# A decoder trunk with split-precision projections: the weights' low half in fp32r in place of bf16

## The chip, the cores and the metric

One core of a Trainium2 chip. The metric is the device time of one execution in microseconds; a kernel is timed as the median of several runs, and one further execution is profiled.

## What is computed

Two layers on one sequence of 256 positions of width 1024, all in float32. Layer 0 puts one input projection in front of two groups of heads (forgetting attention and retention), multiplies their outputs by a gate and projects them back. Layer 1 is sparse attention with a compressed, a selected and a window branch, a gate and an output projection. Each layer starts with an RMS norm and adds its input; a last norm ends it.

```python
h = rms_norm(x, norm_g); u = h @ w_in                      # layer 0
q_f, k_f, v_f, f_l, q_r, k_r, v_r, z = jnp.split(u, EVEN_SPLITS, axis=-1)
...
y = jnp.concatenate([o_f, o_r], axis=-1) * jax.nn.silu(z)
x = x + y @ w_out
...
h = rms_norm(x, norm_g); u = h @ w_in                      # layer 1
q, kc, vc, ks, vs, kw, vw, gl, z = jnp.split(u, ODD_SPLITS, axis=-1)
...
return jax.nn.silu(ab @ w1) @ w2                           # compress_blocks, for keys and for values
...
x = x + (o * jax.nn.silu(z)) @ w_out
```

## The kernel before

**Split products.** Each large product is made of three smaller ones, so that it keeps more digits than one fast product would. An operand is written as a high half (rounded to fp32r, a float32 that TensorE multiplies at a fast rate) and a low half (what the rounding left). The class `Split` holds an activation h so: `h` and `l` in fp32r, and `b`, a bf16 copy of the high half. ScalarE writes `h`, VectorE (for x0 and x1, L119) or GpSimd (for y0 and y1, L102) writes `l`, GpSimd copies `b` (L99). The weights come in 38 chunks of 256 to 280 columns: SyncE loads a chunk (1 MB) into a stage tile `st` (three buffers); `split` cuts it in four quarters, ScalarE rounding each into `wh` (fp32r, L95) and VectorE subtracting it into `wl` (bf16, L102). The product is `wh` with `h`, `wh` with `l` and `wl` with `b`.

**Units.** A chunk holds two units. A unit is one output tile of 128 rows, with 8 slices k of the sum and three matmuls for each: 24 matmuls into one PSUM bank, 256 columns each. `mtile` takes the weights as the stationary operand (matmul at L211), `vtile` the activations (L218). `runs` writes out the order: for `runs(4, 4)` it is `wh` with `h` and `l` for k = 0 to 3, then `wl` with `b` for the same four k, then the same for k = 4 to 7. A unit is handed out in eight steps of three matmuls.

**The order of the work.** `Feed` has the list of all steps; the attention code calls `feed.run(n)` between its own parts, so that TensorE has projection work while the other engines make softmax and norms. The numbers n are written out by hand (`FR`, `RR`, `HW`, `NR` and so on). A chunk's quarters are split when the step counter is within `LEAD` = 22 steps of its start (four steps apart), and the last quarter issues the next load that is free. This program order is then the priority of a list scheduler, which fixes the order on every engine and on SyncE's queue ahead of the run; at run time every engine takes its instructions in that order.

**The turn between the layers.** The output projection of layer 0 (`pp_o`) adds to `xT` (VectorE, L380), from which `put_scaled` makes x1 and `Norm.add` a running sum of squares (`acc_n`, GpSimd). R, the norm's factor, is there when the last tile is summed. Then the compression keys and values follow (`kc`, `vc`): VectorE multiplies by R and writes `ab`, the blocks, in 32 pieces; `ph` (L707) multiplies `ab` with the compression weights `w` in eight rounds of four products, with three feed steps between rounds. Each round needs 256 KB for keys and the same for values: `load_w1` has eight loads of 512 KB into two buffers of their own, the first two ahead of the rounds, the others each after the round that frees a buffer.

Of the kernel before, what the change touches and what calls it, by code (L numbers as in the profile page):

```python
# [25 lines left out]
for _name, _w in (("U", 512), ("onehot", 8), ("mask", 384), ("ident", 128), ("bones", 128),  # L26
# [5 lines left out]
WMAX = 280  # L32
# [12 lines left out]
N0 = (5, 0, 8, 0, 0, 9)  # L45
LEAD = 22

E = dict(whi="AAAA", wlo="VVVV", xhi="AAAAAAAA", x0hi="AAAVAAAV", w0hi="AAAV", xb="G", sq="A", acc="G", yhi="A", ylo="G", yb="G", sz="G",
         q2h="AA", q2l="GG", a0="A", a1="V", ac="V", norm="GGGG", pn="G", kh="AA", kl="VV", ab="VVVV", pT="A", cs="GG", tree="VGG", xg="AAAAAAAA")
FIN = (("V", 0, 1), ("G", 1, 1), ("V", 2, 2), ("G", 4, 1), ("V", 5, 3))  # L50

# [2 lines left out]
def trunk_kernel(ctx: ExitStack, tc: tile.TileContext, a: dict):  # L54
    nc = tc.nc
    V, A, G, T = nc.vector, nc.scalar, nc.gpsimd, nc.tensor
# [36 lines left out]
    def copy(e, o, x):  # L93
        if e == "A":
            A.activation(o, x, AF.Copy)  # L95
        elif e == "V":
            V.tensor_copy(o, x)
        else:
            G.tensor_scalar(o, x, 1.0, 1.0, op0=OP.mult, op1=OP.mult)  # L99
# [11 lines left out]
    class Split:  # L111
        def __init__(s, name, tag):
            s.h = cp.tile([P, KT, S], F32R, tag=tag + "h", name=name + "h")
            s.l = cp.tile([P, KT, S], F32R, tag=tag + "l", name=name + "l")
            s.b = cp.tile([P, KT, S], BF, tag=tag + "b", name=name + "b")

        def put_scaled(s, k, x, g, e="xhi"):
            scale(E[e][k], s.h[:, k], x, g)
            V.scalar_tensor_tensor(s.l[:, k], x, g, s.h[:, k].bitcast(F32), op0=OP.mult, op1=OP.subtract)  # L119
            copy(E["xb"], s.b[:, k], s.h[:, k].bitcast(F32))  # L120

        def put(s, k, y):
            copy(E["yhi"], s.h[:, k], y)
            binary(E["ylo"], s.l[:, k], y, s.h[:, k].bitcast(F32), OP.subtract)
            copy(E["yb"], s.b[:, k], s.h[:, k].bitcast(F32))

# [1 line left out]
    class Feed:  # L130
# [22 lines left out]
        def split(s):  # L153

            i, q = divmod(s.cut, 4)
            c = s.chunks[i]
            n, st = c["n"], c["st"]
            if q == 0:
                c["w"] = (whp.tile([P, KT, WMAX], F32R, tag="wh", name=f"wh{i}"),
                          wlp.tile([P, KT, WMAX], BF, tag="wl", name=f"wl{i}"))  # L160
            wh, wl = c["w"]
            k = slice(2 * q, 2 * q + 2)
            copy(E["whi" if i else "w0hi"][q], wh[:, k, :n], st[:, k, :n])
            binary(E["wlo"][q], wl[:, k, :n], st[:, k, :n], wh[:, k, :n].bitcast(F32), OP.subtract)
            s.cut += 1
            if q == 3 and s.loaded < len(s.chunks):
                s.load()
# [11 lines left out]

    feed = Feed()  # L180

    def runs(*lengths):

        seq, k0 = [], 0
        for n in lengths:
            seq += [(w, k) for k in range(k0, k0 + n) for w in "hl"] + [("b", k) for k in range(k0, k0 + n)]
            k0 += n
        assert k0 == KT
        return seq

    def products(kind, name, done, seq, one):

        def make(c):
            o = []

            def step(i):
                if i == 0:
                    o.append(bank(kind, "pp_" + name))
                for n in range(3 * i, 3 * i + 3):
                    one(c, o[0], *seq[n], n == 0, n == 3 * KT - 1)  # L200
                if i == KT - 1:
                    done(c, o[0])
            return step
        return make

    def mtile(col, xs, kind, name, done, seq=runs(4, 4)):

        def one(c, p, w, k, start, stop):
            x = xs() if callable(xs) else xs
            wt = c["w"][w == "b"]  # L210
            T.matmul(p[:, :S], wt[:, k, col * P:col * P + P], dict(h=x.h, l=x.l, b=x.b)[w][:, k], start=start, stop=stop)  # L211
        return products(kind, name, lambda c, p: done(p[:, :S]), seq, one)

    def vtile(tt, x, kind, name, done, seq=runs(4, 4)):

        def one(c, p, w, k, start, stop):
            wt, n = c["w"][w == "b"], c["n"]
            T.matmul(p[:, :n], dict(h=x.h, l=x.l, b=x.b)[w][:, k, tt * P:tt * P + P], wt[:, k, :n], start=start, stop=stop)  # L218
        return products(kind, name, lambda c, p: done(p[:, :c["n"]]), seq, one)

    class Norm:

# [114 lines left out]
    def forget_sum():  # L337
# [5 lines left out]
        for i in (32, 96):  # L343
            V.tensor_tensor(CC[i:i + 8], pc[i:i + 8, :S], CC[i:i + 8].bitcast(F32), op=OP.subtract)

    feed.chunk(a["w0v0"], 264, [vtile(tt, x0, "p", f"v0_0{tt}", v0_done(0, tt), runs(*[1] * KT)) for tt in range(2)],
               [(tt, k) for k in range(KT) for tt in range(2)])
    for c in range(1, 4):
        feed.chunk(a["w0c"][c - 1], 256, [vtile(tt, x0, "s" if c == 1 else "p", f"v0_{c}{tt}", v0_done(c, tt)) for tt in range(2)])
# [35 lines left out]
    def out_chunks(w, y, done, nm, wide, early):  # L385

        units = []
        for m in range(8):
            units.append(mtile(m % 2, y, "p" if m < 2 or m >= wide else "s", f"{nm}{m}", done(m),
                               runs(*((4, early - 4, 8 - early) if m < wide else (4, 4)))))  # L390
        start = len(feed.steps)
        for c in range(4):
            feed.chunk(w[c], 256, units[2 * c:2 * c + 2])
        st = feed.steps[start:]
        step = lambda m, k: st[m * 8 + k]
        order = [(m, k) for m in range(wide) for k in range(early)]
        order += [(m, k) for k in range(early, 8) for m in range(wide)]
        order += [(m, k) for m in range(wide, 8) for k in range(8)]
        feed.steps[start:] = [step(m, k) for m, k in order]
        for c in range(4):  # L400
            feed.chunks[-4 + c]["start"] = start + min(i for i, (m, k) in enumerate(order) if m // 2 == c)
# [64 lines left out]
    def v1_done(c, tt):  # L466
        def done(p):
# [4 lines left out]
            if tt == 1:  # L472
# [2 lines left out]
                V.tensor_scalar(g0, g0, C("rowm"), None, op0=OP.mult)  # L475
        return done

    feed.chunk(a["w1c"][0], 256, [mtile(0, x1, "s", "kc0", c00_done, runs(4, 3, 1)), mtile(1, x1, "s", "kc1", c_done(0, 1), runs(4, 3, 1))],
               [(u, k) for u in range(2) for k in range(7)] + [(0, 7), (1, 7)])
    feed.chunk(a["w1c"][1], 256, [mtile(u, x1, "p", f"vc{u}", c_done(1, u)) for u in range(2)])  # L480
    feed.chunk(a["w1c"][2], 256, [mtile(u, x1, "s", f"ks{u}", ks_done(0, u)) for u in range(2)])
# [29 lines left out]
            v1_chunk(1)  # L511
            feed.steps += q1_steps

    y1 = Split("y1", "y")
    x2 = xT

    def o1_done(m):
# [156 lines left out]
    sq = None  # L674
# [19 lines left out]
    w1 = {}  # L694

    def load_w1(i):
        w1[i] = wk.tile([P, 2, 2, 256], F32, tag="w1", name=f"w1_{i}")
        nc.sync.dma_start(w1[i], a["wkv1"][:, :, 2 * i:2 * i + 2].rearrange("v p j n -> p v j n"))

    load_w1(0)  # L700
    load_w1(1)
# [2 lines left out]
    for qr in range(8):  # L704
        for j in range(2):
            for kv in range(2):
                T.matmul(ph[64 * kv:64 * kv + 64, :256], ab[:, kv, 2 * qr + j].rearrange("p g c -> p (g c)"),  # L707
                         w1[qr][:, kv, j], start=(qr == 0 and j == 0), stop=(qr == 7 and j == 1))
        if qr < 6:
            load_w1(qr + 2)  # L710
        feed.run(HW[1 + qr])
    hid = wk.tile([P, 256], F32, tag="y", name="hid")
    hs = wk.tile([P, 256], F32, tag="kc", name="hs")
# [21 lines left out]
    for u in range(2):  # L735
# [266 lines left out]
```

## Time and profile before

| | us |
|---|---|
| median of 3 runs | 320.18 (318.6 to 321.68) |
| the profiled execution: its time | 321.15 |
| its span, from the first instruction to the last | 319.4 |
| TensorE busy | 301.4 |
| VectorE busy | 226.6 |
| ScalarE busy | 202.5 |
| GpSimd busy | 125.2 |

Busy times are unions of an engine's instructions; matmuls overlap in the pipeline, so a high busy share of TensorE doesn't say how fast the matmuls follow each other. The mean granted clock of TensorE is 0.984 of 2.4 GHz. PE is TensorE, PEld its weight loads, DVE VectorE, ACT ScalarE, POOL GpSimd, SP SyncE.

### The profile page before, as it was taken

What the parts mean: (1) busy time and instruction counts of PE and PEld (TensorE: products, weight loads), DVE (VectorE), ACT (ScalarE), POOL (GpSimd) and SP (SyncE); (2) the same over time, 40 slices, a digit from 0 to 9 for tenths busy, and PEclk for the clock granted to TensorE, in tenths of its full rate; (3) what the DMA queues carried; (4) which work ended last, traced back from release to release, by engine and by line L of the source; (5) the groups of instructions that cost most, each with busy time, mean ns of one, the idle gap of its engine ahead of it and who ended that gap; (6) DMA issues with size and microseconds to landing.
All of it is one profiled execution on the core that took longest, in us unless ns stands there. A gap on an engine that the chain in (4) does not pass through costs nothing.

```text
span 319.4 us, 6788 instructions
## 1 busy us (share of the span) xinstructions
PE 301.4 (94%) x2478; PEld 263.4 (82%) x2478; DVE 226.6 (71%) x686; ACT 202.5 (63%) x547; POOL 125.2 (39%) x202
## 2 busy tenths in 40 slices
PE   6989999999999999999959989999999999999990
PEld 4879988988888888988947767997998899888980
DVE  2988955665656555299998937798978898883433
ACT  4759456666645456287425628598988898891461
POOL 2520020542423115284100000367778777973242
PEclk9799999999999999999997999999999999999997
DMA  6997799754343433408717992226322442100003
GB/s 178 365 308 248 262 389 307 250 174 133 131 134 131 134 133 133 131 6 269 263 29 253 303 331 73 84 70 196 133 63 72 135 131 68 67 2 0 3 0 131
DMA packets 43137, 49.72 MB, mean 156 GB/s; under 512 B 1632, under 2 KB 39776, under 8 KB 42848
## 3 DMA queue, kind: packets, MB, share of 16 engines
q1 hardware_dynamic: 42816, 49.03, 46.9%
q8 instruction: 19, 0.31, 0.4%
q10 hardware_dynamic: 288, 0.26, 0.2%
q14 instruction: 14, 0.11, 0.1%
HBM read 48.24 MB, written 1.05 MB: 154 GB/s over the span
## 4 chain that ended last, share of the span: by engine, by line
PE 54%; DVE 21%; ACT 15%; DMA 4%; issue 3%; POOL 1%; DVEq 0%; SPq 0%; ACTq 0%; POOLq 0%
PE pp_o L211 10%; ACT p L782 9%; PE pp_q L211 8%; DVE wl L102 7%; PE pp_k L211 7%; PE pp_z L211 7%; PE pp_v L218 5%; DVE ab L102 3%; PE ph L707 2%; DMA w<-in_wkv_dram 2%; PE pp_kc L211 2%; PE pp_kw L211 2%; ACT wh L95 2%; ACT q L95 2%; DMA xT<-in_xT_dram 1%
## 5 line engine op out<-in xcount | busy, mean ns | idle before, releaser
L102 DVE TENSOR_TENSOR wl<-st,wh 128x512 bf16<-128x512 f32 (+2 forms) x152 | 107.2, 736 | 10.3 <-ACT wh L95 9.7
L95 ACT ACTIVATE wh<-st 128x512 fp32r<-128x512 f32 (+2 forms) x151 | 87.7, 621 | 37.9 <-PE pp_o L211 8.1
L108 POOL TENSOR_SCALAR p<-p,st 128x128 f32<-128x128 f32 (+1 forms) x80 | 44.7, 576 | 49.5 <-DVE st L598 31.2
L211 PEld LDWEIGHTS <-wl 128*128 128x128 bf16 x512 | 40.1, 98 | 11.1 <-issue 2.1
L782 ACT ACTIVATE p<-ns,st 128x128 f32<-128x128 f32 (+1 forms) x64 | 28.4, 445 | 7.7 <-DVE st L770 7.6
L102 POOL TENSOR_TENSOR q<-q,q 64x256 fp32r<-64x256 f32 x16 | 12.1, 756 | 48.2 <-ACT q L95 47.2
L218 PE MATMUL pp_v<-wh,x0h 128*128 128x256 f32 (+1 forms) x64 | 19.9, 337 | 1.9 <-ACT wh L95 1.9
L770 DVE CUSTOM_DVE_ANT_0 ns<-s,cst 128x128 f32<-128x128 f32 (+1 forms) x64 | 20.1, 350 | 0.0
L211 PE MATMUL pp_o<-y0h,wh 128*128 128x256 f32 x64 | 17.8, 308 | 0.7 <-DVE xT L380 0.7
L211 PE MATMUL pp_z<-x0h,wh 128*128 128x256 f32 x64 | 18.1, 309 | 0.0
L211 PE MATMUL pp_q<-x0h,wh 128*128 128x256 f32 x64 | 17.7, 308 | 0.0
L211 PE MATMUL pp_q<-x1h,wh 128*128 128x256 f32 x64 | 17.6, 303 | 0.0
L211 PE MATMUL pp_k<-x0h,wh 128*128 128x256 f32 x64 | 17.2, 302 | 0.0
L218 PE MATMUL pp_v<-wh,x0l 128*128 128x256 f32 (+1 forms) x64 | 17.0, 291 | 0.0
L211 PE MATMUL pp_o<-y1h,wh 128*128 128x256 f32 x64 | 16.9, 303 | 0.0
L211 PE MATMUL pp_o<-y1l,wh 128*128 128x256 f32 x64 | 16.9, 289 | 0.0
L211 PE MATMUL pp_z<-x0l,wh 128*128 128x256 f32 x64 | 16.6, 286 | 0.0
L211 PE MATMUL pp_z<-x1h,wh 128*128 128x256 f32 x64 | 16.6, 292 | 0.0
L211 PE MATMUL pp_q<-x1l,wh 128*128 128x256 f32 x64 | 16.1, 280 | 0.0
L211 PE MATMUL pp_o<-y0l,wh 128*128 128x256 f32 x64 | 16.1, 281 | 0.0
L211 PE MATMUL pp_q<-x0l,wh 128*128 128x256 f32 x64 | 16.0, 280 | 0.0
L211 PE MATMUL pp_k<-x0l,wh 128*128 128x256 f32 x64 | 15.9, 281 | 0.0
(322 smaller groups left out, 907.1 us busy)
## 6 DMA issues: line engine op xcount, KB each, us to landing
st<-in_w0c_dram SPq DMA_DIRECT2D x13, 1024.0 KB, 5.7
st<-in_w1c_dram SPq DMA_DIRECT2D x12, 1024.0 KB, 5.7
w<-in_wkv_dram SPq DMA_DIRECT2D x8, 512.0 KB, 5.7
st<-in_w0o_dram SPq DMA_DIRECT2D x4, 1024.0 KB, 5.7
st<-in_w1o_dram SPq DMA_DIRECT2D x4, 1024.0 KB, 5.5
st<-in_w1v_dram SPq DMA_DIRECT2D x2, 1120.0 KB, 5.0
st<-in_w0c_dram SPq DMA_DIRECT2D x4, 512.0 KB, 8.1
dec<-in_dec_dram SPq DMA_DIRECT2D x2, 768.0 KB, 8.8
```

What stands on the lines that cost most here:

```text
L95: A.activation(o, x, AF.Copy)
L102: (V if e == "V" else G).tensor_tensor(o, x, y, op=op)
L108: (V if e == "V" else G).tensor_scalar(o, x, c, 1.0, op0=OP.mult, op1=OP.mult)
L211: T.matmul(p[:, :S], wt[:, k, col * P:col * P + P], dict(h=x.h, l=x.l, b=x.b)[w][:, k], start=start, stop=stop)
L218: T.matmul(p[:, :n], dict(h=x.h, l=x.l, b=x.b)[w][:, k, tt * P:tt * P + P], wt[:, k, :n], start=start, stop=stop)
L707: T.matmul(ph[64 * kv:64 * kv + 64, :256], ab[:, kv, 2 * qr + j].rearrange("p g c -> p (g c)"), w1[qr][:, kv, j], start=(qr == 0 and j == ...
L770: V.tensor_tensor_reduce(out=out, in0=pp[:, lo:lo + n], in1=C(tab, lo, lo + n), scale=-slope, scalar=3e38, op0=OP.add, op1=OP.min, accum_o ...
L782: A.activation(p[:, d:d + n], ns[:, d:d + n], AF.Exp, scale=-1.0, bias=st[:, qt, br, 0:1], accum_out=st[:, qt, br, 1:2])
```

## The change

The bf16 copies are gone: `Split` has `h` and `l` alone, `wl` becomes an fp32r tile of the same shape, and the third product multiplies `wl` with `h`. All three operands of a k are multiplied one after the other (`hh`, `hl`, `lh`), and `runs` is gone with its groups of four. The compression weights come in four loads of 1 MB. They have no buffers of their own any more: loads 0 and 2 take the buffer of `y0h` (and later `y1h`), loads 1 and 3 that of `y0l`; `y1` is declared after them.

```diff
 class Split:
-            s.b = cp.tile([P, KT, S], BF, tag=tag + "b", name=name + "b")
...
         def put_scaled(s, k, x, g, e="xhi"):
             scale(E[e][k], s.h[:, k], x, g)
             V.scalar_tensor_tensor(s.l[:, k], x, g, s.h[:, k].bitcast(F32), op0=OP.mult, op1=OP.subtract)
-            copy(E["xb"], s.b[:, k], s.h[:, k].bitcast(F32))
 
         def put(s, k, y):
             copy(E["yhi"], s.h[:, k], y)
             binary(E["ylo"], s.l[:, k], y, s.h[:, k].bitcast(F32), OP.subtract)
-            copy(E["yb"], s.b[:, k], s.h[:, k].bitcast(F32))
...
-                          wlp.tile([P, KT, WMAX], BF, tag="wl", name=f"wl{i}"))
+                          wlp.tile([P, KT, WMAX], F32R, tag="wl", name=f"wl{i}"))
...
-    def products(kind, name, done, seq, one):
+    def products(kind, name, done, one):
...
-                for n in range(3 * i, 3 * i + 3):
-                    one(c, o[0], *seq[n], n == 0, n == 3 * KT - 1)
+                for n, (w, x) in enumerate(("hh", "hl", "lh")):
+                    one(c, o[0], c["w"][w == "l"], x, i, i == n == 0, i == KT - 1 and n == 2)
...
     def load_w1(i):
-        w1[i] = wk.tile([P, 2, 2, 256], F32, tag="w1", name=f"w1_{i}")
-        nc.sync.dma_start(w1[i], a["wkv1"][:, :, 2 * i:2 * i + 2].rearrange("v p j n -> p v j n"))
+        w1[i] = cp.tile([P, 2, 4, 256], F32, tag=("yh", "yl")[i % 2], name=f"w1_{i}")
+        nc.sync.dma_start(w1[i], a["wkv1"][:, :, 4 * i:4 * i + 4].rearrange("v p j n -> p v j n"))
...
-                         w1[qr][:, kv, j], start=(qr == 0 and j == 0), stop=(qr == 7 and j == 1))
-        if qr < 6:
-            load_w1(qr + 2)
+                         w1[qr // 2][:, kv, 2 * (qr % 2) + j], start=(qr == 0 and j == 0), stop=(qr == 7 and j == 1))
+        if qr in (1, 3):
+            load_w1(qr // 2 + 2)
         feed.run(HW[1 + qr])
...
     feed.run(24 - sum(HID) + HID[2])
+
+    y1 = Split("y1", "y")
```

## Rows read from the trace of the kernel before

**Rows 1.** The page, part 1: busy us (share of the span), instructions.

```profile
PE 301.4 (94%) x2478; PEld 263.4 (82%) x2478; DVE 226.6 (71%) x686; ACT 202.5 (63%) x547; POOL 125.2 (39%) x202
```

**Rows 2.** Stretches: length, busy us of each engine, PEclk, DMA share, GB/s.

```profile
core 0: us, PE busy (x) PEld busy (x) DVE busy (x) ACT busy (x) POOL busy (x), PEclk, DMA share, GB/s
30.00:86.00 56.00, 56.00 (x487) 50.04 (x485) 36.84 (x103) 34.98 (x89) 16.17 (x25) 1.00 0.71 239
134.00:148.00 14.00, 13.30 (x113) 12.27 (x112) 13.89 (x24) 11.34 (x26) 8.62 (x11) 1.00 0.31 88
148.00:168.00 20.00, 16.67 (x134) 14.73 (x134) 19.75 (x50) 8.66 (x19) 3.40 (x4) 1.00 0.52 172
168.00:200.00 32.00, 30.74 (x233) 23.51 (x230) 22.66 (x56) 18.78 (x48) 0.92 (x2) 0.95 0.73 240
```

**Rows 3.** TensorE in order of time, inside a unit: start us, us.

```profile
45.28 0.28 PE L211 MATMUL pp_k<-x0l,wh 128*128 128x256 f32 x1
...
45.99 0.28 PE L211 MATMUL pp_k<-x0l,wh 128*128 128x256 f32 x1
```

**Rows 4.** The chain of waits, one unit of 24: start us, us, what.

```profile
45.32 2.81 PE pp_k L211 x24
```

**Rows 5.** Groups by form, weight loads: busy us, mean ns of one.

```profile
L211 PEld LDWEIGHTS <-wl 128*128 128x128 bf16 x512 | 40.1, 98 | 11.1 <-issue 2.1
...
L211 PEld LDWEIGHTS pp_z<-x0h,wh 128*128 128x128 f32 x64 | 12.1, 189 | 0.3
```

**Rows 6.** TensorE in order of time where it stood still [idle before], and 147.1.

```profile
17.70 0.27 PE L218 MATMUL pp_v<-wl,x0b 128*128 128x256 bf16 x1 [0.78 <-DVE wl L102]
...
144.28 0.38 PE L211 MATMUL pp_o<-y0h,wh 128*128 128x256 f32 x1 [0.69 <-DVE xT L380]
...
147.10 0.36 PE L211 MATMUL pp_kc<-x1h,wh 128*128 128x256 f32 x1
...
167.79 2.38 PE L707 MATMUL ph<-w,ab 128*64 128x256 f32 x14 [3.33 <-DVE ab L102]
...
190.17 1.08 PE L707 MATMUL ph<-w,ab 128*64 128x256 f32 x8 [1.26 <-DMA w<-in_wkv_dram]
```

**Rows 7.** The stretch behind the longest stop; columns as in rows 2.

```profile
169.00:173.00 4.00, 4.00 (x22) 2.91 (x19) 3.09 (x7) 1.51 (x4) 0.00 (x0) 0.57 0.85 278
```

**Rows 8.** Groups by form on VectorE and GpSimd: busy us, mean ns.

```profile
L119 DVE SCALAR_TENSOR_TENSOR x1l<-xT,gv,x1h 128x256 fp32r<-128x256 f32 x8 | 5.4, 699 | 0.0
...
L119 DVE SCALAR_TENSOR_TENSOR x0l<-xT,gv,x0h 128x256 fp32r<-128x256 f32 x8 | 4.3, 580 | 5.1 <-ACT x0h L106 5.1
...
L492 DVE SCALAR_TENSOR_TENSOR q<-pp_q,cst,R_n 128x256 f32<-128x256 f32 x8 | 3.8, 474 | 0.0
...
L102 DVE TENSOR_TENSOR sq<-sq 128x1024 f32<-128x1024 f32 x1 | 1.2, 1212 | 0.0
...
L99 POOL TENSOR_SCALAR y1b<-y1h 128x256 bf16<-128x256 f32 x8 | 3.2, 406 | 0.0
```

**Rows 9.** VectorE and GpSimd in order of time: start us, us.

```profile
13.12 0.47 DVE L119 SCALAR_TENSOR_TENSOR x0l<-xT,gv,x0h 128x256 fp32r<-128x256 f32 x1
...
148.08 0.83 POOL L99 TENSOR_SCALAR x1b<-x1h 128x256 bf16<-128x256 f32 x1 [1.52 <-ACT x1h L106]
...
148.57 0.61 DVE L119 SCALAR_TENSOR_TENSOR x1l<-xT,gv,x1h 128x256 fp32r<-128x256 f32 x1
...
161.45 0.68 DVE L102 TENSOR_TENSOR wl<-st,wh 128x512 bf16<-128x512 f32 x1
```

**Rows 10.** SyncE's queue of transfers in order of time.

```profile
52.88 0.94 SPq L698 DMA_DIRECT2D w<-in_wkv_dram  x2
...
165.64 0.34 SPq L148 DMA_DIRECT2D st<-in_w1v_dram  x1
```

**Rows 11.** The page, part 6: transfers, KB each, median us to landing.

```profile
w<-in_wkv_dram SPq DMA_DIRECT2D x8, 512.0 KB, 5.7
...
st<-in_w1c_dram SPq DMA_DIRECT2D x12, 1024.0 KB, 5.7
```

More of the change, by code (lines that the diff above doesn't have):

```diff
@@ L46 @@
 LEAD = 22
-E = dict(whi="AAAA", wlo="VVVV", xhi="AAAAAAAA", x0hi="AAAVAAAV", w0hi="AAAV", xb="G", sq="A", acc="G", yhi="A", ylo="G", yb="G", sz="G",
+E = dict(whi="AAAA", wlo="VVVV", xhi="AAAAAAAA", x0hi="AAAVAAAV", w0hi="AAAV", sq="A", acc="G", yhi="A", ylo="G", sz="G",
          q2h="AA", q2l="GG", a0="A", a1="V", ac="V", norm="GGGG", pn="G", kh="AA", kl="VV", ab="VVVV", pT="A", cs="GG", tree="VGG", xg="AAAAAAAA")
@@ L180, in trunk_kernel @@
     feed = Feed()
[L182 to L189, printed above, removed]
-    def products(kind, name, done, seq, one):
+    def products(kind, name, done, one):
         def make(c):
@@ L204, in products, with mtile, one, vtile @@
         return make
[L206 to L219, printed above, removed]
+    def mtile(col, xs, kind, name, done):
+        def one(c, p, wt, x, k, start, stop):
+            xp = getattr(xs() if callable(xs) else xs, x)
+            T.matmul(p[:, :S], wt[:, k, col * P:col * P + P], xp[:, k], start=start, stop=stop)
+        return products(kind, name, lambda c, p: done(p[:, :S]), one)
+    def vtile(tt, xs, kind, name, done):
+        def one(c, p, wt, x, k, start, stop):
+            n = c["n"]
+            T.matmul(p[:, :n], getattr(xs, x)[:, k, tt * P:tt * P + P], wt[:, k, :n], start=start, stop=stop)
+        return products(kind, name, lambda c, p: done(p[:, :c["n"]]), one)
     class Norm:
@@ L344, in forget_sum @@
             V.tensor_tensor(CC[i:i + 8], pc[i:i + 8, :S], CC[i:i + 8].bitcast(F32), op=OP.subtract)
-    feed.chunk(a["w0v0"], 264, [vtile(tt, x0, "p", f"v0_0{tt}", v0_done(0, tt), runs(*[1] * KT)) for tt in range(2)],
+    feed.chunk(a["w0v0"], 264, [vtile(tt, x0, "p", f"v0_0{tt}", v0_done(0, tt)) for tt in range(2)],
                [(tt, k) for k in range(KT) for tt in range(2)])
@@ L388, in out_chunks @@
         for m in range(8):
-            units.append(mtile(m % 2, y, "p" if m < 2 or m >= wide else "s", f"{nm}{m}", done(m),
-                               runs(*((4, early - 4, 8 - early) if m < wide else (4, 4)))))
+            units.append(mtile(m % 2, y, "p" if m < 2 or m >= wide else "s", f"{nm}{m}", done(m)))
         start = len(feed.steps)
@@ L476, in v1_done @@
         return done
-    feed.chunk(a["w1c"][0], 256, [mtile(0, x1, "s", "kc0", c00_done, runs(4, 3, 1)), mtile(1, x1, "s", "kc1", c_done(0, 1), runs(4, 3, 1))],
+    feed.chunk(a["w1c"][0], 256, [mtile(0, x1, "s", "kc0", c00_done), mtile(1, x1, "s", "kc1", c_done(0, 1))],
                [(u, k) for u in range(2) for k in range(7)] + [(0, 7), (1, 7)])
@@ L512, in trunk_kernel @@
             feed.steps += q1_steps
-    y1 = Split("y1", "y")
     x2 = xT
```

## Prediction, made before the result

> **What bounds the kernel now.** I read the page's busy shares first: TensorE 94% of the span, every other engine well below [rows 1]. A busy share is an average, so the next view is the stretches [rows 2]. From 30 to 86 us TensorE is busy the whole time, with 487 matmuls in 56 us; this is a stream, and the same holds up to about 134 us. From 134 to 168 us VectorE is busy 33.6 of 34 us while TensorE has 4 us to spare: this stretch belongs to VectorE. From 168 to 200 us TensorE is nearly full again, but at a granted clock of 0.95. The third view is TensorE in order of time, at each place where it stood still [rows 6]: 0.78 us for `wl` at 17.7, 0.69 us behind `xT` at 144.3, 3.33 us for `ab` at 167.8, 1.26 us for a transfer of `w` at 190.2. Right after the longest of these the clock is 0.57 over four microseconds [rows 7], which means that some of that time ran at 1.2 instead of 2.4 GHz; before it the engine had been idle for 3.33 us. So there are two prices to find: what the change does to the pace of the matmul stream, and what it does to these four stops and the slow clock.
>
> **The pace of the products.** There are 76 units (output tiles of a projection) of 24 matmuls each: 16 in fp32r, 8 in bf16. The change makes all 24 fp32r. The nearest rows are inside one unit: from the second fp32r matmul at 45.28 to the eighth at 45.99 six starts pass in 0.71 us, 0.1183 us each [rows 3]. In this run the weights stay for a pair and then change, so both cases of the new order (same weights, other weights) are in the number. A whole unit of today takes 2.81 us in the chain of waits, just after [rows 4]. New unit: 24 x 0.1183 = 2.84 us, so +0.03 us a unit. Rounding of the rows (0.71 +- 0.01) puts the pace between 0.1167 and 0.120, and the unit between 2.80 and 2.88: from nothing to +0.07 us. Below nothing is excluded, since the third product has the very shape and types of the other two. Chunks 0 to 18 (38 units) run before or around 134 us: +1.1 us. The next seven units lie in VectorE's stretch, with idle time on TensorE to hide them: 0. The last 31 units: +0.9 us. Sum +2.0 us, bounds 0 and +4.8 (69 units x 0.07).
>
> One rule of the Trainium skill speaks against the change. First the rows: a bf16 weight load takes 98 ns, an fp32r one 189 ns [rows 5]. "TensorE: Matmul & The Clock Gate", section "Weight-path perf modes", says that fast weight load is only on where the type is not FP32, and the section "Back-to-back issue gap" that loads and matmuls together set the spacing. By the one the new products cost 55 us (rival 4), by the other what the pace above gives. Today's fp32r matmuls follow each other at 0.118 us although each load takes 0.189 us [rows 3, 5], so here the loads overlap; the rule is kept as a rival of little weight.
>
> **The low half in fp32r on VectorE.** The same 152 subtractions, with a 4-byte result. 128x512 into bf16 takes 0.68 us alone [rows 9]. No row shows it into fp32r; the nearest are a sum of 1024 columns into f32 at 1212 ns [rows 8] and 256 columns of `x0l` into fp32r at 0.47 us [rows 9]: (1212 - 474) / 768 = 0.96 ns a column, so 512 columns would take 0.72 us by the line through both, and about 0.6 us by half of the longer one. I take no change; bounds -0.08 and +0.04 us each. It matters only where VectorE sets the pace (some 20 of them between 134 and 168 us): -1.6 to +0.8 us.
>
> **The casts that go.** 32 GpSimd copies of 128x256 (`x0b`, `x1b`, `y0b`, `y1b`) fall away; GpSimd isn't near a bound, so their own time gives nothing. What they cost is on VectorE. Alone `x0l` takes 0.47 us; beside `x1b` an `x1l` took 0.61 us [rows 9]; over all eight, `x0l` has a mean of 580 and `x1l` of 699 ns against 474 for the same operation in the attention part [rows 8]. At the start that is 8 x 0.106 = 0.85 us before the second chunk's `wl`, for which TensorE waits 0.78 us at 17.7: I take -0.7, between 0 (the transfers of the stage tiles hold it instead) and -0.8. In VectorE's stretch I take 8 x 0.14 = -1.1 us; the upper end is that all of 699 - 474 goes, -1.8; the lower end is +0.5, if the running sum `acc_n`, which follows on GpSimd, now falls onto `wl` one more time. TensorE resumes at 167.8 when the last `ab` is written, so this lands in the time in full. What is late next is still VectorE.
>
> A second rule is "SBUF — State Buffer", section "SBUF: two separate sides": a VectorE instruction with two inputs in SBUF and a GpSimd instruction exclude each other, and the one that began first keeps the other out for its whole length. By it each `x1b` that came first would have held VectorE for its own time, 406 ns for the like copy `y1b` [rows 8], so 3.2 us for eight. The row shows the other order as well: `x1b` took 0.83 us, beside `wl` and `x1l` [rows 9], so GpSimd did much of the waiting. The sum keeps 1.1; the 3.2 belongs to the first rival.
>
> **The order inside a unit.** Today `wl` is first used after eight fp32r matmuls, after the change behind two, so up to 0.7 us earlier. None of the stops after the first is for `wl` [rows 6], and in the steady part the low halves are made a chunk ahead (`LEAD`, 22 steps of about 0.35 us). I take nothing, except at the start, where the second chunk's first unit follows VectorE closely; that is why 0.7 and not 0.85 stands above.
>
> **The compression weights.** Today two of eight 512 KB loads are issued at 52.9 us [rows 10], long ahead, and six follow as the matmuls of `ph` free a buffer; one of them is what the 1.26 us stop waits for. After the change the first two of four 1 MB loads go into the buffers of `y0h` and `y0l`, so they wait for the last matmul of the first output projection, which ends as `kc` starts at 147.1 [rows 6]. A load of 1 MB lands 5.7 us after its issue at the median [rows 11]: 11.4 us for two one behind the other, 17.1 if a stage load is still ahead of them, so 158.5 to 164.2, before the first use in earnest at 167.8: no cost. Queued behind the two on SyncE are the stage loads of 150 us and later, that of 165.64 [rows 10] among them; a stage tile is split many steps after it is loaded, which covers a few us. If that cover were gone they would be late by the time that the two take, 11.4 us, and that is a case near the third rival. The other two loads follow rounds two and four of `ph`; today every pair of rounds makes one trip to memory, so three trips lie in the chain of eight rounds, and then there are two, the second begun while the first is on its way. TensorE fills such gaps with projection steps, so only the stop itself is paid back: -1.3 us (bounds 0 and -1.3).
>
> **The slow clock.** The stop of 3.33 us shrinks: VectorE is 1.1 us earlier and TensorE's own work ahead of it is 0.2 us longer, so about 2 us stay. The stretch after it lost (1 - 0.57) x 4 = 1.7 us of full clock [rows 7]. Whether the clock still falls after a shorter stop no row shows; I take half, -0.8, bounds 0 and -1.7.
>
> **The sum.** -0.7 + 1.1 - 1.1 + 0.9 - 1.3 - 0.8 = -1.9 us. The profiled execution took 321.15 us (span 319.4 and 1.75 around it), so 319.2; the median of the runs is 0.97 us below it: 320.18 - 1.9 = 318.3 us. A difference of 1% (3.2 us) is about what a measurement of this kernel can tell from none.
>
> **The rivals.**
> 1. All stops close: start -0.8, VectorE -1.8 to -3.2, transfer -1.3, the clock -1.7, pace +1.4. About -5: 315.2 us. For it: VectorE's stretch ends in one wait, and everything ahead of it is one chain. Against: `acc_n` stays and slows `wl` as today. Chance 0.30.
> 2. Only the pace counts: the stops re-form behind other things (`wl` that is needed earlier, R of the norm, which comes just before `kc`). +2.0 us: 322.2. For it: TensorE is 94% busy. Chance 0.20.
> 3. The first compression weights come too late. SyncE issues in order; if the first 1 MB load stands behind the stage load of 165.64 [rows 10], it lands 5.7 us later [rows 11] where the two move side by side, 11.4 where one follows the other: 171.3 to 177.0, in the middle 174.2. TensorE, which holds to its order, would stand 6.4 us longer than until today's 167.8 (both ends move along with VectorE's stretch). It decides from a landing later than `ab`. -1.9 + 6.4 + 0.8 (the clock falls all the same) = +5.3: 325.5 us. Against: the buffers are free at 147.1, with three stage loads between. Chance 0.10.
> 4. Weight loads set the pace of the third product: 608 matmuls at 0.189 instead of 0.098 us [rows 5], +55 us: 375 us. Chance 0.02.
>
> **How the numbers follow.** The forecast has 0.38; its own range is 316.8 to 320. Faster by over 1% (below 317.0): rival 1 and a little of the forecast, 0.34. Slower by over 1% (above 323.4): rivals 3 and 4 and the upper end of rival 2, 0.15. Within 1%: 0.51. The range reaches from 314.8 (rival 1) to 323.2: rival 2 with a third more of its pace bound; the rest of that bound, rivals 3 and 4 and the lowest of rival 1 are left out.
>
> **What would show it.** Pace: a unit of 24 takes 2.84 us in an undisturbed stretch at 45 us. Casts: `x1l` falls to about 0.55 us, and `ab` ends about a microsecond sooner after the first `xT` of the output projection. Weights: two loads issued at about 148 us, landed before 160, and no stop of `ph` for `w`. Clock: 1.00 in the four microseconds behind the stop at 167. The prediction is wrong if units take another time than 2.80 to 2.88 us, if TensorE waits for `wl` in the steady part, or if `ph` waits for its first weights.

## The result, and the profile after

The change makes the kernel slower: 324.49 us (median of 4 runs, 323.17 to 326.39) against 319.99 of the kernel before; the ratio on record is 1.0128, with an interval of 1.0086 to 1.0169 (the two medians alone would give 1.0141). The forecast was 318.3, between 314.8 and 323.2.

The profiled execution after took 323.17 us, with a span of 321.4, against 321.15 and 319.4. So the two traces hold 2.0 of some 4 us; the first experiment bears on the rest. First the page, parts 1 and 6:

```profile
PE 303.9 (95%) x2478; PEld 280.8 (87%) x2478; DVE 224.0 (70%) x686; ACT 202.9 (63%) x547; POOL 107.8 (34%) x170
...
w<-in_wkv_dram SPq DMA_DIRECT2D x4, 1024.0 KB, 6.4
```

TensorE is busy for 2.5 us longer, VectorE for 2.6 us and GpSimd for 17 us less [rows 1]. The weight loads, 263.4 us before, take 280.8. Next, TensorE in order of time after the change: the places where it stands still, and the first rows of four parts of the program (the first scores of layer 0, the last product of retention, the first scores of layer 1, the last norm).

```profile
19.32 0.61 PE L243 MATMUL pc_n<-ones,acc_n 128*128 128x1 f32 x4 [0.74 <-POOL acc_n L102]
...
42.53 0.39 PE L564 MATMUL s<-CC,sel 40*128 40x256 f32 x2
...
124.70 0.65 PE L598 MATMUL por<-at,vt 128*64 128x256 f32 x4
...
168.19 2.62 PE L692 MATMUL ph<-w,ab 128*64 128x256 f32 x14 [3.27 <-DVE ab L102]
...
190.21 0.44 PE L705 MATMUL pth<-cst,hid 128*128 128x128 f32 x2 [0.37 <-DVE hid L701]
...
201.66 0.39 PE L746 MATMUL s<-KH,q 128*128 128x272 f32 x1 [2.12 <-POOL q L102]
...
311.86 0.59 PE L234 MATMUL pn_n<-acc_n,ones 128*128 128x256 f32 x2
```

And the same four marks in the kernel before (the row of `ph` stands in [rows 6]):

```profile
42.56 0.39 PE L579 MATMUL s<-CC,sel 40*128 40x256 f32 x2
...
123.51 0.65 PE L613 MATMUL por<-at,vt 128*64 128x256 f32 x4
...
199.72 0.29 PE L759 MATMUL s<-KH,q 128*128 128x272 f32 x1
...
309.98 0.60 PE L247 MATMUL pn_n<-acc_n,ones 128*128 128x256 f32 x2
```

The same work lies between the marks in both kernels (for the fourth stretch 230 and 231 matmuls are recorded, for the fifth 940 and 938). Subtracting mark from mark gives the table that everything below refers to:

| stretch, us | before | after | change |
|---|---|---|---|
| start to first scores | 42.56 | 42.53 | -0.03 |
| to the last retention product | 80.95 | 82.17 | +1.22 |
| to `ph` behind the wait for `ab` | 44.28 | 43.49 | -0.79 |
| to the first scores of layer 1 | 31.93 | 33.47 | +1.54 |
| to the last norm | 110.26 | 110.20 | -0.06 |
| to the end | 9.42 | 9.54 | +0.12 |

Three of the four old stops are gone, those for `wl`, `xT` and `w` [rows 6]. The fourth and longest is as long as it was (3.27 for 3.33 us). Three are new: 0.74 us for `acc_n`, the sum for the norm, 0.37 for `hid`, and 2.12 for `q`. The pace is what the forecast said: the chain of waits shows a unit of 24 at 2.82 to 2.85 us, here the one at the place of [rows 4], though its third products load weights for 189 ns each (groups by form), where bf16 took 98 [rows 5].

```profile
45.30 2.83 PE pp_k L198 x24
```

```profile
L198 PEld LDWEIGHTS pp_k<-x0h,wl 128*128 128x128 f32 x64 | 12.1, 189 | 0.0
```

The clock falls behind the wait for `ab` as before: the same four microseconds, columns as in [rows 2], against 0.57 in [rows 7].

```profile
169.00:173.00 4.00, 4.00 (x21) 2.76 (x19) 3.94 (x8) 1.54 (x4) 0.00 (x0) 0.57 0.57 173
```

### The profile page after: what moved, and what is told of

It is laid out like the page before. It is cut to its first block, busy times and chain, and to the rows that moved or that the text cites. A ratio compares the mean times of both kernels' runs of the same rounds, so it can differ in the third digit from the quotient of the medians.

```text
span 321.4 us, 6747 instructions
## 1 busy us (share of the span) xinstructions
PE 303.9 (95%) x2478; PEld 280.8 (87%) x2478; DVE 224.0 (70%) x686; ACT 202.9 (63%) x547; POOL 107.8 (34%) x170
## 4 chain that ended last, share of the span: by engine, by line
PE 82%; DVE 8%; ACT 4%; POOL 2%; DMA 1%; issue 1%; DVEq 0%; SPq 0%; ACTq 0%; POOLq 0%
PE pp_o L198 14%; PE pp_z L198 14%; PE pp_q L198 14%; PE pp_k L198 7%; PE pp_v L205 6%; PE po L825 4%; DVE ab L102 3%; PE ptA L796 2%; PE ph L692 2%; PE s L746 2%; PE s L747 2%; PE pp_kc L198 2%; PE pp_kw L198 2%; DMA xT<-in_xT_dram 1%; ACT wh L95 1%; POOL sq L102 1%
## 5 line engine op out<-in xcount | busy, mean ns | idle before, releaser
L102 DVE TENSOR_TENSOR wl<-st,wh 128x512 fp32r<-128x512 f32 (+2 forms) x152 | 103.8, 714 | 10.8 <-ACT wh L95 8.7
L108 POOL TENSOR_SCALAR p<-p,st 128x128 f32<-128x128 f32 (+1 forms) x80 | 42.6, 548 | 50.0 <-DVE st L583 31.3
L198 PE MATMUL pp_z<-x1h,wh 128*128 128x256 f32 x64 | 18.6, 291 | 0.0
L205 PE MATMUL pp_v<-wl,x0h 128*128 128x256 f32 (+1 forms) x64 | 18.3, 297 | 0.0
L198 PE MATMUL pp_o<-y1h,wl 128*128 128x256 f32 x64 | 18.1, 282 | 0.0
L198 PE MATMUL pp_q<-x1l,wh 128*128 128x256 f32 x64 | 18.1, 282 | 0.0
L198 PE MATMUL pp_z<-x1l,wh 128*128 128x256 f32 x64 | 18.0, 282 | 0.0
L198 PE MATMUL pp_z<-x1h,wl 128*128 128x256 f32 x64 | 18.0, 281 | 0.0
L198 PE MATMUL pp_q<-x0h,wl 128*128 128x256 f32 x64 | 18.0, 281 | 0.0
L198 PE MATMUL pp_k<-x0l,wh 128*128 128x256 f32 x64 | 18.0, 281 | 0.0
```

The lines of the kernel that those rows point to most:

```text
L102: (V if e == "V" else G).tensor_tensor(o, x, y, op=op)
L108: (V if e == "V" else G).tensor_scalar(o, x, c, 1.0, op0=OP.mult, op1=OP.mult)
L198: T.matmul(p[:, :S], wt[:, k, col * P:col * P + P], xp[:, k], start=start, stop=stop)
L205: T.matmul(p[:, :n], getattr(xs, x)[:, k, tt * P:tt * P + P], wt[:, k, :n], start=start, stop=stop)
```

## The experiments

Each is one edit to the kernel after the change or to the one before. Ratios are those on record, to the kernel before on the same chip; 0.001 is 0.32 us. The medians alone give slightly other numbers (for e8 0.9886). With the widths of the intervals, a difference between two runs is uncertain by 0.9 to 1.6 us.

| run | ratio | interval |
|---|---|---|
| e1 after, unedited | 1.0119 | 1.0079 to 1.0158 |
| e2 before, four large loads | 1.0050 | 1.0021 to 1.0078 |
| e3 after, eight loads | 1.0071 | 1.0043 to 1.0099 |
| e4 after, scores later | 1.0055 | 1.0028 to 1.0083 |
| e5 after, casts kept | 1.0139 | 1.0110 to 1.0168 |
| e6 after, norm's sum on VectorE | 1.0086 | 1.0057 to 1.0115 |
| e7 after, scores and `ph` later | 0.9953 | 0.9919 to 0.9987 |
| e8 before, large loads, scores and `ph` later | 0.9863 | 0.9831 to 0.9895 |
| e9 before, scores and `ph` later | 0.9950 | 0.9921 to 0.9979 |
| e10 as e8, `ph` later still | 0.9933 | 0.9900 to 0.9967 |
| e11 after, groups of four | 1.0183 | 1.0143 to 1.0222 |
| e12 as e7, `ph` later still | 1.0020 | 0.9994 to 1.0047 |
| e13 after, first cast kept | 1.0111 | 1.0070 to 1.0152 |
| e14 after, last cast kept | 1.0116 | 1.0075 to 1.0157 |
| e15 as e7, first cast kept | 0.9955 | 0.9924 to 0.9986 |

### The same kernel again, and the two halves of the change

**e1_after_again**, no edit.

> The changed kernel once more, unedited, for a second profile and a narrower interval. Both theories: 4 to 4.5 us over the kernel before (ratio 1.012 to 1.014). In its profile a unit of 24 takes 2.84 us, the first scores of the sparse attention wait about 2 us for q, and the clock falls after the stop at 168 us.

324.23 us (323.26 to 325.21). The ten executions of the changed kernel, these six and the first four, form two groups: five from 323.17 to 323.50, with a mean granted clock of 0.981 to 0.987, and five from 324.96 to 326.39, at 0.976 to 0.978. The profile after is of the first group, this one of the second: TensorE's row of the first scores, and the window from 20 to 24 us.

```profile
44.40 0.39 PE L564 MATMUL s<-CC,sel 40*128 40x256 f32 x2
```

```profile
20.00:24.00 4.00, 4.00 (x22) 3.95 (x23) 1.64 (x4) 3.41 (x9) 0.00 (x0) 0.65 0.86 289
```

The first scores come at 44.40 instead of 42.53; the four stretches behind them are 82.17, 43.48, 33.43 and 110.19 us, the table's numbers within 0.04. So between these two profiles the whole difference lies in the start: here the stop for `acc_n` took 1.47 us, and a clock of 0.65 followed it. The other executions have no trace, and the place can be another. Three later profiles, e5, e6 and e14 (324.68 to 325.67 us), have their first scores at 42.47 to 43.39 and take 111.70 to 111.73 us for the fifth stretch instead of 110.20; the granted clock there is below 1.00 (200 to 300 us, columns as in [rows 2], e5 and then e6), while it is 1.00 from 200 to 286 us in the profile after:

```profile
200.00:300.00 100.00, 98.32 (x824) 92.12 (x825) 76.41 (x344) 76.99 (x249) 68.29 (x119) 0.98 0.27 85
```

```profile
200.00:300.00 100.00, 98.33 (x824) 92.11 (x825) 76.41 (x344) 76.99 (x249) 65.68 (x112) 0.98 0.27 85
```

As far as the mean clocks and these profiles show, the groups differ by one more stretch at a low clock, wherever it lies. As an estimate, this closes the gap between traces and medians: +2.0 of the traces, +0.9 (half of the executions are 1.9 later), and 0.35 to 1.2 because the profiled execution of before lay above its medians of 320.8 and 319.99: 3.3 to 4.1 us.

**e2_loads_only** takes the loads' part of the change alone, bf16 and casts kept; **e3_eight_loads** takes all but that, with eight 512 KB loads as before, in the buffers of y:

```diff
 # e3, against the kernel after
     def load_w1(i):
-        w1[i] = cp.tile([P, 2, 4, 256], F32, tag=("yh", "yl")[i % 2], name=f"w1_{i}")
+        w1[i] = cp.tile([P, 2, 2, 256], F32, tag=("yh", "yl")[i % 2], name=f"w1_{i}")
...
-        if qr in (1, 3):
-            load_w1(qr // 2 + 2)
+        if qr < 6:
+            load_w1(qr + 2)
```

> The kernel before with the four 1 MB compression loads of the change alone; the low half stays bf16, all casts stay. Pace theory (the new matmul pace costs about 2 us, the loads trade one stop for another): the stop of 1.26 us for w goes, one of about 2 us for q and one of 0.4 us for hid come, so +1.2 us (ratio 1.004). Loads theory (the rearranged compression work is most of the loss): +3 us or more (ratio 1.009 or more). If the loads are a gain by themselves: -1.3 us.

> The changed kernel with eight loads of 512 KB, as before the change, but in the buffers of y: fp32r low half, no casts, and TensorE's order around the compression as before. Pace theory: +2.5 us against before (ratio 1.008), units of 2.84 us, no stop of 2 us for q, the stop for w back at about 1.3 us. Loads theory: within 1 us of the kernel before.

322.19 and 322.55 us. By the ratios the loads cost 0.5%, the fp32r half 0.7%, and together they make the 1.2%. e2 has no stop for `w` any more, and a stop for `q` instead (TensorE in order of time):

```profile
201.12 0.39 PE L760 MATMUL s<-KH,q 128*128 128x272 f32 x1 [2.28 <-POOL q L102]
...
310.10 0.60 PE L247 MATMUL pn_n<-acc_n,ones 128*128 128x256 f32 x2
```

From the scores to the last norm e2 takes 108.98 us and the changed kernel 110.20, in the same order: +1.22 us, the price of the pace in that stretch. The traces of e2 and of the kernel before differ by only 0.2 us (spans of 319.6 and 319.4). From the wait for `ab` to the scores e2 is 1.26 us longer (33.19 for 31.93); behind them it is 1.28 us shorter (108.98 for 110.26), since TensorE waits less among the attention's matmuls there (the kernel before stands 0.39 us for `ac` at 220.9, e2 does not). So the -0.06 in the table is 1.22 us of pace less 1.28 of such waits, and the 1.6 us that the loads cost in the runs of e2 are not located by these two traces. In fp32r the traces do show a price: the changed kernel takes 33.47 + 110.20 us for the two stretches, e3 31.18 + 110.58, 1.91 us less. e3 has neither the stop for `w`, which was expected back at 1.3 us, nor the one for `q`; why `w` does not stop it is not shown.

**e4_scores_later** moves the first scores of layer 1 back by four steps.

```diff
-N0 = (5, 0, 8, 0, 0, 9)
+N0 = (9, 0, 4, 0, 0, 9)
```

> The changed kernel with the first scores placed four steps (12 matmuls, 1.4 us) later. Both theories: the stop for q shrinks from 2.1 us to about 0.7; the time falls by 1.4 us against the changed kernel if that stop is paid in full, by nothing if the attention's softmax chain starts late instead and costs it further on.

321.94 us, 0.0064 (2.1 us) below e1; the stop for `q` is 0.59 (and one of 0.86 for `w` is back, in `ph`):

```profile
202.15 0.39 PE L746 MATMUL s<-KH,q 128*128 128x272 f32 x1 [0.59 <-POOL q L102]
```

That shows that the 2.12 us hang on the place of the scores in the order. The traces show the rest. With the new loads the fixed order puts the compressed keys (`pth`, `pkc`, `pz`) ahead of unit `q_0` instead of behind it, and the first scores 15 matmuls behind `q_0`. The last matmul of `q_0` starts at 197.34 us; VectorE, still at the compressed keys and two `wl` behind them, comes to its `q` at 199.35, GpSimd makes the low half of `q` last, and TensorE waits for that (after the change):

```profile
199.35 0.48 DVE L478 SCALAR_TENSOR_TENSOR q<-pp_q,cst,R_n 128x256 f32<-128x256 f32 x1
```

```profile
200.42 2.00 POOL L102 TENSOR_TENSOR q<-q,q 64x256 fp32r<-64x256 f32 x2 [47.94 <-ACT q L95]
```

In the kernel before VectorE is at `q` 2.9 us sooner, and the compressed keys' 16 matmuls `pkc` and `pz` still stand between `q_0` and the scores:

```profile
196.48 0.48 DVE L492 SCALAR_TENSOR_TENSOR q<-pp_q,cst,R_n 128x256 f32<-128x256 f32 x1
```

### The start, the casts and the order in a unit

**e5_casts_kept** puts the 32 casts back, into tiles that nobody reads.

```diff
...
+            copy("G", s.b[:, k], s.h[:, k].bitcast(F32))
...
```

> The changed kernel with GpSimd's 32 casts put back; they write bf16 tiles that nobody reads, so the products stay fp32r. It prices the casts alone. By the prediction they cost 0.7 us at the start and 1.1 us in VectorE's stretch between 134 and 168 us: 324.4 + 1.8 = 326.2. By what the trace after the change shows (the sum acc_n, not the casts, ends the wait at the start; the wait for ab ends 0.8 us earlier relative to the work ahead of it): +0.8, 325.2, with the stop for ab longer by that. If VectorE only waits for GpSimd where TensorE has slack: 324.4, and the stop for ab as long as without the casts.

325.75 us; against e1 +0.0020 (0.6 us), and the intervals overlap. In the trace, the stretch to `ph` takes 44.50 us instead of 43.49 (from 125.26 to 169.76), so the casts cost 1.0 us there. At the start they cost nothing that lasts: first scores at 43.09, between those of the two profiles above. But they decide who is first there. GpSimd and VectorE in order of time, first with the casts, then without them (the profile after):

```profile
15.27 1.66 POOL L102 TENSOR_TENSOR sq<-sq 128x512 f32<-128x512 f32 x1 [2.51 <-DVE sq L102]
17.01 1.06 POOL L102 TENSOR_TENSOR acc_n<-sq 128x256 f32<-128x256 f32 x1
...
15.11 4.11 DVE L102 TENSOR_TENSOR wl<-st,wh 128x512 fp32r<-128x512 f32 x4
```

```profile
14.39 4.07 POOL L102 TENSOR_TENSOR sq<-sq 128x512 f32<-128x512 f32 x1 [13.46 <-DVE sq L102]
18.54 0.72 POOL L102 TENSOR_TENSOR acc_n<-sq 128x256 f32<-128x256 f32 x1
...
14.22 2.50 DVE L102 TENSOR_TENSOR wl<-st,wh 128x512 fp32r<-128x512 f32 x4
```

With the casts GpSimd's addition `sq` takes 1.66 us, and VectorE's four `wl` beside it and the following `acc_n` take 4.11 instead of 2.50. One by one, the first `wl` takes 0.68 us, the second, beside `sq`, 1.77, and the third, beside `acc_n`, 1.22: VectorE loses 1.1 us to the one addition and 0.5 to the other. Without the casts VectorE runs through and `sq` takes 4.07. Its end sets `acc_n`, which TensorE needs next: 19.26 us, against 18.24 in the kernel before, where both engines' times are those of e5.

"SBUF — State Buffer" of the Trainium skill, section "SBUF: two separate sides", says that of a VectorE operation with two inputs in SBUF and a GpSimd operation the one that starts first has the shared port for its whole length. The trace of e5 agrees: `sq`, issued at 15.27, ends 1.1 us after the end of the first `wl` (15.79 to 16.93), and the second `wl` is longer by as much. That `sq` waits through four operations and a cast of VectorE in the profile after is not in the rule.

**e6_norm_tree** gives the two additions to VectorE.

```diff
...
-         ... tree="VGG", ...
+         ... tree="VVV", ...
```

> The changed kernel with the last two additions of the first norm's sum on VectorE in place of GpSimd (tree VVV for VGG). Theory: after the change the wait at the start is no longer for wl but for that sum (0.7 to 1.5 us at 17 to 19 us); with the sum earlier the stop closes and the time falls by about 1 us to 323.4, with x0l and wl unchanged. Rival: the two additions (256 and 512 columns, some 0.9 us on VectorE) delay wl, the old stop for wl is back, and the time stays at 324.4 within 0.5.

323.95 us, 0.0033 (1.1 us) below e1, about what the theory said, but the intervals overlap. In the trace the stop for `acc_n` is gone and TensorE stands 0.75 us for `fl`, an operation of VectorE right behind:

```profile
22.98 0.39 PE L205 MATMUL pp_v<-wh,x0h 128*128 128x256 f32 x1 [0.75 <-DVE fl L294]
```

The first scores come at 42.47 there, earlier than in e1 (44.40) but as in the profile after (42.53).

**e13_first_cast_kept** and **e14_last_cast_kept** keep one of the casts (k == 0 or k == 7), to see whether GpSimd is slow because `sq` is its first operation.

```diff
+            if e == "x0hi" and k == 0:
+                copy("G", cp.tile([P, S], BF, tag="unread", name="unread"), s.h[:, k].bitcast(F32))
...
```

> The changed kernel with one of GpSimd's 32 casts put back, that of the first slice of x0 at about 8 us, into a tile that nobody reads. After the change GpSimd's addition sq takes 4.07 us beside four wl and a cast of VectorE, and is the first thing GpSimd does since its memset at the start; with the casts kept the same addition took 1.66 us and got in after the first wl. Theory 1 (GpSimd is slow in its first operation): with one cast ahead of it sq takes 1.66 us again, VectorE's four wl take 4.1 us, acc_n ends about a microsecond earlier, the stop of pc_n closes, and the time falls by 0.7 to 2 us (the slow clock behind the stop goes too): 323. Theory 2 (the port was VectorE's and GpSimd was held out for as long as VectorE had work with two inputs): sq still takes 3.5 to 4.1 us and the time stays at 324.4 within 0.5.

> As e13_first_cast_kept, but with the cast of the last slice of x0, at about 12.5 us, just ahead of the addition. Theory 1: the same, sq 1.66 us, about 323. Theory 2: only a GpSimd that is at work when VectorE's sq ends would get the port; as the cast ends before that (0.5 us from 12.5), sq takes 3.5 to 4.1 us and the time stays at 324.4. If only this run and not the other shows 1.66, what counts is how lately GpSimd was at work.

324.68 and 324.61 us. `sq` takes 4.06 and 4.05 us, and `acc_n` stops TensorE for 1.47 and 1.46. The first-operation theory falls. With the eight casts of x0 kept GpSimd gets in after the first `wl`, with one or none it doesn't; what decides that stays open.

**e11_groups_of_four** has the old order inside a unit, with fp32r.

> The changed kernel with the old order inside a unit: four slices of wh with h and l, then the same four of wl with h (and the old other groups where the kernel before had them). It tests the prediction's step that the order inside a unit is worth nothing. By that: 324.4 within 0.7, the pace 0.118 us a matmul as without it. If the order matters because wl is needed earlier: 323.5 or less, and the stop for wl or acc_n at 18 us is shorter. If pairs with the same weights are what keeps the pace at 0.118: the third products, which now change weights and activations both, follow at 0.12 or more, and the time rises by 1 us or more.

327.24 us, 0.0064 above e1. Neither reason that I had given is it. From the first scores (45.11) to the last retention product (127.25) it takes 82.14 us, as the changed kernel does, so the pace there doesn't depend on the order. What differs in the start is one stop: from 8 us on the trace shows 57 matmuls ahead of the norm's, 73 in the kernel after, and TensorE waits for the same `acc_n` for 3.05 us:

```profile
18.69 0.61 PE L253 MATMUL pc_n<-ones,acc_n 128*128 128x1 f32 x4 [3.05 <-POOL acc_n L102]
```

Against the trace of e1 this makes the start 0.7 us longer (45.11 for 44.40). The fourth stretch is 1.2 us longer (34.65 for 33.43) behind an equal stop for `ab` (3.27 for 3.24), and the granted clock there is lower (0.72 and 0.50 in the four microseconds from 168 and from 172, against 0.92 and 0.65); that part is not traced to the order.

### The wait for `ab`, and what the parts are worth without it

**e7_ph_later** and **e8_bf16_ph_later** have the later scores and begin `ph` eight steps later; e7 is the changed kernel, e8 the one before with the large loads alone.

```diff
-HW = (40, 3, 3, 3, 3, 3, 3, 3, 3)
+HW = (48, 2, 2, 2, 2, 2, 2, 2, 2)
```

> The changed kernel with the scores four steps later (as in the run before) and the rounds of ph begun eight steps later (HW 48 and eight times 2 in place of 40 and eight times 3), so that 24 projection matmuls more lie ahead of the first round. Theory: the stop for ab (3.3 us) shrinks to about 0.5 and the clock does not fall behind it, another 1 to 1.7 us: 321.9 - 2.8 - 1.3 = 317.8, between 317 and 319. Rival: VectorE is the bound there, and the time that TensorE saves comes back as waits for wl, kf or q at 170 to 205 us: 321.5 to 322. A second one: the rounds now follow each other so closely that the third and fourth load are late; a stop for w of 2 us or more, 319.5 to 320.5.

> The kernel before, bf16 low half and casts and all, with only the four 1 MB loads in the buffers of y, the scores four steps later and the rounds of ph eight steps later. Against the run with ph later it differs by the fp32r half alone. If fp32r costs only its pace (69 units of 0.03 us, 2.1 us) it is 2.1 us faster than that run: about 315.7 where that gives 317.8. If the casts cost VectorE 0.8 us or more where it is the bound, the difference is 1.3 us or less.

319.56 and 317.29 us: the later rounds give 0.0102 (3.3 us) against e4, or 2.4 us by the two traces (spans of 317.9 and 320.3), and e8 beats both kernels by more than 1%. The stop for `ab` is about half as long in both, not the 0.5 us that was expected. TensorE in order of time (first e7, then e8):

```profile
168.56 0.65 PE L692 MATMUL ph<-w,ab 128*64 128x256 f32 x4 [1.73 <-DVE ab L102]
```

```profile
167.50 1.08 PE L706 MATMUL ph<-w,ab 128*64 128x256 f32 x6 [1.77 <-DVE ab L102]
```

e7 and e8 differ by 0.0090 (2.9 us; 2.3 by the medians), the fp32r half. Within the uncertainty that is the 2.1 of its pace; that it is more is not shown.

**e9_own_buffers** is e8 with the eight old loads in their own buffers.

> The kernel before with the scores four steps later and the rounds of ph eight steps later, and nothing else: eight 512 KB loads in buffers of their own, bf16 and casts as they were. Against e8_bf16_ph_later it differs by the loads alone. If the four large loads are worth the stop for w that they close (1.3 us) once their own new stops are paid back, this run is 1.3 us or more above that one: about 318.6, with a stop for w. If their only effect is to move the work behind ph, which the later scores had already answered: within 0.5 us of 317.3, and no stop for w above 0.3.

319.4 us, 0.0087 (2.8 us; 1.9 by the medians) above e8. `ph` stands 1.31 us for `w`:

```profile
182.40 1.08 PE L707 MATMUL ph<-w,ab 128*64 128x256 f32 x8 [1.31 <-DMA w<-in_wkv_dram]
```

Behind the scores e9 takes 108.42 us to the last norm and e8 107.50. So the same four loads that cost 1.6 us in e2 are worth 2 to 3 us once the scores and the rounds of `ph` have moved; which of the two moves decides that was not tried apart.

**e10_bf16_ph_last** and **e12_fp32r_ph_last** begin `ph` later still.

```diff
+HW = (54, 0, 3, 0, 3, 0, 2, 0, 2)
```

> e8_bf16_ph_later with the rounds of ph begun six steps later still, so that 18 more projection matmuls (2.1 us) lie ahead of the first round. Theory: the rest of the stop for ab (1.77 us) closes, and the clock has nothing to fall behind: 317.3 - 1.8 = 315.5. Rival: with pth and the compressed keys now inside q_0, q and the scores are late again (stop of 2 us for q at 198): 317 to 317.5. If VectorE stands behind TensorE for the whole stretch, the stop goes to kf or wl: the same.

> The changed kernel with the schedule of e10_bf16_ph_last. Against that run it differs by the fp32r half alone, as e7_ph_later does against e8_bf16_ph_later (2.3 to 2.9 us). If the half costs its pace (2.1 us) and gives back the casts (1.0 us) only where VectorE sets the end, then with the stop for ab closed TensorE sets the end and the difference is 2 us or more: about 317.6. If the casts count here too, 1 us: 316.6.

318.91 and 321.77 us, by the ratios slower than e8 and e7. The stop for `ab` is closed, and TensorE stands for the third load instead. In e10 (TensorE, then SyncE's queue):

```profile
182.72 3.68 PE L706 MATMUL ph<-w,ab 128*64 128x256 f32 x16 [3.77 <-DMA w<-in_wkv_dram]
```

```profile
174.15 0.56 SPq L148 DMA_DIRECT2D st<-in_w1c_dram  x1
174.81 1.11 SPq L697 DMA_DIRECT2D w<-in_wkv_dram  x2
```

In e8 that load was issued at 170.54, ahead of a stage load at 172.90:

```profile
170.54 0.38 SPq L697 DMA_DIRECT2D w<-in_wkv_dram  x1
172.90 0.56 SPq L148 DMA_DIRECT2D st<-in_w1c_dram  x1
```

In e10 the 16 matmuls of `ph` that free its buffer end at 170.27, but the load stands in SyncE's order behind the stage load of 174.15. Neither expectation had this. e12 is 0.0087 (2.8 us) above e10. So four pairs give the price of the fp32r half, each within 0.9 to 1.6 us: 2.2 us (e1 against e2), 2.3 (e3 against before), 2.9 (e7, e8) and 2.8 (e12, e10); by the medians alone 2.0, 1.8, 2.3 and 2.9.

**e15_fp32r_best** is e7 with the one cast.

> e7_ph_later with the one cast of e13_first_cast_kept: the changed kernel with every stop answered that the runs found an answer for. Theory 1: 0.7 to 2 us below e7 (0.9953 of the kernel before): 317.6 to 318.8 where the kernel before takes 321, a ratio of 0.990 to 0.993, so that it still stands 1 us or more behind e8_bf16_ph_later (0.9863), which pays no price in pace. Theory 2: 0.995.

319.42 us, as e7; the same stop for `acc_n`, 1.46 us.

## Why the prediction was wrong

The terms, in the prediction's order, against the table and the runs:

**Pace.** Forecast +2.0, and right in its mechanism: 2.84 us a unit, weight loads hidden, no stop for `wl` in the steady part. It measured +1.22 up to 124 us and +1.22 from the scores on (e2), so about 2.4. The term that was too small lacks the price of starting again behind the attention's matmuls. Taken from end to end of neighbouring matmuls (the ends are modelled), the 503 steps from product to product up to 124 us took 0.59 us more in all, about the 0.03 us a unit of the forecast, and the 22 steps from the attention to a product 0.63 us more. Rows of TensorE at one such place, before and after: behind `po` the fifth product starts 0.46 us behind the first where the first three are in bf16 (67.38 to 67.84), and 0.58 in fp32r (67.59 to 68.17); the forecast had no price for that place.

```profile
67.06 0.39 PE L615 MATMUL po<-pT,vt 128*64 128x128 f32 x4
67.38 0.50 PE L211 MATMUL pp_q<-x0b,wl 128*128 128x256 bf16 x3
67.64 0.37 PE L211 MATMUL pp_k<-x0h,wh 128*128 128x256 f32 x1
67.84 0.28 PE L211 MATMUL pp_k<-x0l,wh 128*128 128x256 f32 x1
```

```profile
67.27 0.39 PE L600 MATMUL po<-pT,vt 128*64 128x128 f32 x4
67.59 0.39 PE L198 MATMUL pp_q<-x0h,wh 128*128 128x256 f32 x1
...
68.05 0.28 PE L198 MATMUL pp_k<-x0h,wh 128*128 128x256 f32 x1
68.17 0.28 PE L198 MATMUL pp_k<-x0l,wh 128*128 128x256 f32 x1
```

**VectorE's stretch.** Forecast -1.1, measured -0.79, and 1.0 by e5. The place was another: `x1l` did not fall to 0.55 us but rose from 699 [rows 8] to 783 ns. With `x1b` gone `acc_n` meets `x1l` (at 148.65 and 148.78 us after the change) instead of `wl` (148.88 and 149.11 before), and the 20 `wl` of that stretch fell from a mean of 810 to 699 ns. VectorE's operations of 134 to 169 us, by form, before and after:

```profile
L102 DVE TENSOR_TENSOR wl<-st,wh 128x512 bf16<-128x512 f32 x20 | 15.6, 810 | 0.0
```

```profile
L102 DVE TENSOR_TENSOR wl<-st,wh 128x512 fp32r<-128x512 f32 x20 | 13.4, 699 | 0.3 <-ACT wh L95 0.3
...
L118 DVE SCALAR_TENSOR_TENSOR x1l<-xT,gv,x1h 128x256 fp32r<-128x256 f32 x8 | 6.1, 783 | 0.0
```

That a 128x512 result in fp32r costs VectorE nothing was right: 0.69 us each at the start (2.50 for four).

**The start, forecast -0.7: the first step that failed.** The stop for `wl` closed as said. But the sum for the norm, which came in early in every profile with the casts, came 1.0 us later, and TensorE waited for that: 0.0 us against before in the profile after, +1.9 in that of e1. Rival 2 had named the norm, though at the other end of the layer.

**The compression weights, forecast -1.3: the second.** The loads were early enough, landed in 6.4 us and closed the stop for `w`, as forecast. What came next was not looked up: the fixed order, planned anew, moved the compressed keys ahead of `q_0`, and VectorE and GpSimd were not ready. New stops: 0.37 + 2.12 us, and the stretch measured +1.54. By the runs the loads cost 1.6 us (e2 against before) where -1.3 was forecast, though the two traces of that pair show only 0.2. e9 against e8 shows that the term itself was right in sign, and too small (2 to 3 us), where the schedule behind it gives room.

**The slow clock, forecast -0.8: the third.** The stop was to shrink to 2 us and shrank by 0.06: what VectorE gained also closed the wait for `xT` (0.69 us [rows 6]), so TensorE came to the stop sooner by nearly as much as `ab` did. The clock fell to 0.57 again. That it falls behind a stop is not fixed either: in e5 the stop was as long (3.27 us) and the clock stayed at 1.00 from 168 to 200 us.

So it was rival 2, stops that form again behind other things, and its +2.0 was too low since it counted nothing for them. By the terms the fp32r half alone would have cost +0.2 us (-0.7 + 2.0 - 1.1); four pairs of runs give 2.2 to 2.9 (1.8 to 2.9 by the medians).

Open is what lets GpSimd in at the start and what decides whether the clock falls there, behind `ab` or behind `q`. The traces find some 2.4 us of pace and give 0.8 to 1.0 back on VectorE, so 1.4 to 1.6; the pairs of runs lie above that, but each within its uncertainty, so a further cost is not shown. If there is one, the start may hold it; no run separates it.

## What to carry to other kernels

A stop that closes is worth its length only up to the next wait in the same engine's order; before booking it, go down that order and ask for each operand when it will be there, above all where a planner makes the order anew. The same four loads cost 1.6 us in one order and gave 2 to 3 in another, and a step count moved by four paid about 2. When an engine's work is taken away, ask whom it had held up: the one that follows may now collide with something more urgent.

## What the runs showed of the hardware

- The granted clock did not fall behind every stop, nor by the stop's length alone: 0.57 behind 3.27 us of waiting in the profile after, 0.60 behind 1.73 us in e7, and 1.00 behind 1.77 us in e8, over the same four microseconds (169 to 173); in e5 it was 1.00 behind 3.27 us. At the start it was 0.65 from 20 to 24 us behind 1.47 us in e1 and 1.00 behind 1.47 us in e13. In e8:

```profile
169.00:173.00 4.00, 4.00 (x32) 2.53 (x31) 3.95 (x9) 3.92 (x10) 0.00 (x0) 1.00 0.44 126
```

- fp32r weight loads of 189 ns each, one for every matmul, overlap with the matmuls: these follow each other every 0.118 us (24 in 2.83 us), where 16 in fp32r and 8 in bf16, whose loads take 98 ns, took 2.81.
- A GpSimd addition of 128x512 took 1.66 or 4.07 us beside the same four subtractions of VectorE, which took 4.11 (with a second, smaller addition beside them) or 2.50: one of the two engines waits for the other.
